# Hybrid decoder layer: the token-major projection and HGRN2 moved ahead of the delta rule, the sample states as moving operands

## The chip, the core and the metric

The kernel runs on one core of one Trainium2 chip. The metric is device time in microseconds of one execution. Five engines work beside each other and wait for one another by semaphores: PE (matrix multiply, with its weight loads PEld), DVE (vector), ACT (scalar and activation), POOL (GpSimd) and SP, which here only issues transfers. Each engine runs its own instructions in a fixed order: an instruction that waits holds up all behind it.

## What is computed

One layer for a prompt of 1024 tokens and for 8 samples of 4 tokens, with the same weights, 1056 tokens in all:

```python
h = rmsnorm(x);  z = h @ w_in          # columns: q k v | a b | out gate A | q f i | out gate B | two branch gates
qkv = silu(causal_conv(q, k, v))       # branch A, gated delta rule, 4 heads of 128 x 128
for chunk:  u = T(v*beta) - T(k*beta*exp(G)) @ S;  o = q*exp(G) @ S + attn @ u;  S = S*exp(Gl) + k^T u
for chunk:  o = q*exp(B) @ S + attn(q, k, decay per channel) @ i                 # branch B, HGRN2
            S = S*exp(Bl) + k^T i
y = per-head rmsnorm(o) * silu(out gate) @ w_branch                              # for A and for B
x += (sigmoid(ga)*y_a + sigmoid(gb)*y_b) @ w_out
x += (silu(conv(h2 @ w_gate)) * (h2 @ w_up)) @ w_down;   rmsnorm
```

T is the inverse of a lower triangular matrix for each chunk of tokens and each head. Each sample starts from its own state S (128 x 128 for each head, 8 samples), and the new states are outputs.

## The kernel before, in words

Dense products are made in three matmuls that keep f32 accuracy: every operand is split into a high and a low part (`split`, lines 82 to 84: a cast on ACT, a subtraction on DVE), and `mm3` (L109 to L111) adds high x high, high x low and low x high. A *dense step* is one call of the fill queue: it fills one bank of PSUM with 24 such matmuls (8 slices of the 1024 features), 352 tokens wide, and evacuates it. `pd` are the banks of dense products, `pm` those of all else. Names that end in hi and lo are the two parts: `hhi`, `hlo` the normed input with features on partitions, `whi`, `wlo` weights, `ohi`, `olo` the two branches' outputs.

The program has these stages.

1. Start. x comes tile by tile (128 tokens), is normed (`norm`: ACT square, DVE, a power on POOL, DVE) and turned by PE transposes (`to_cm`, L186). The first two q/k projections and the a/b columns (`ab_block`, 16 output rows) are made between these tiles.
2. The rest of q, k, v, as dense steps (`fill.drain`).
3. The delta rule in 4 groups of 256 tokens (`gdn_group`), each with two chunks of 128 tokens for 4 heads. A group is a chain: transposes (L694), decay and Gram matrices (L715, L723), which give `UA`; a trip of UA's diagonal blocks through DRAM (`dU`, then `Db`); a forward substitution of 31 dependent pairs of DVE instructions (L749, L751); a second trip through DRAM (`dX`, then `Yd`, transposed to `Xd`); the assembly of T (L773 to L801); two chunk steps on the state (L817 to L835); the head norm (`head_post`, L597 to L612), and a store of the result to `oT_d`.
4. HGRN2 in 4 groups (`hgrn_group`), each a chain of seven levels (`hgrn_attn`: small matmuls L976 or L963, a masked copy on DVE, a product on DVE and one on POOL, then the next level).
5. The dense rest: branch projections, `w_out`, the FFN. It begins with loads of `raw` from `oT_d` (L1151) and splits into `ohi` and `olo`, which lie where `hhi` and `hlo` lay.

In stages 3 and 4 the generators yield numbers, and `drive` runs that many dense steps from the queue `fill` before it goes on. So out gates, HGRN2's projections, the token-major projection of i (`ib_work`, tokens on partitions) and the 16 branch gates lie between the steps of a chain. The samples' own delta rule and HGRN2 run beside the prompt's as a side generator. `sample_products` multiplies each sample's state with its few columns: the state (128 x 128, f32) is the stationary operand, 4 or 8 columns move (L629).

The order in which instructions are written is not the order in which they run: a scheduler orders each engine's instructions by the priority of the writing order, and takes a later one forward where by its own estimate the engine would stand idle. So dense steps are pulled ahead into the long waits.

Of the kernel before, what the change touches and what calls it, by code (L numbers as in the profile page):

```python
# [42 lines left out]
def hybrid_step(ctx: ExitStack, tc: tile.TileContext, ins, outs):  # L43
# [227 lines left out]
    wab = ini.tile([P, KD, 16], F32R, name="wab")  # L271
    rab = ini.tile([P, KD, 8], F32, name="rab")
# [14 lines left out]
    load_x(0)  # L287
    nc.sync.dma_start(out=g_bc, in_=I["g_attn"].broadcast_to([P, D]))
    load_x(1)
    load_x(2)  # L290
    for t in range(3):
        norm1(t)
    W0 = load_w([[(KD, w_in[:, c:c + P])] for c in (OFF_K, OFF_Q)])
    load_x(3)
    load_x(4)
    load_x(5)
    nc.sync.dma_start(out=rab, in_=w_in[:, OFF_AB:OFF_AB + 8].rearrange("(k p) n -> p k n", p=P))
    split(wab[:, :, 0:8], wab[:, :, 8:16], rab)
    abT = ini.tile([16, T], F32, name="abT")

    def ab_block(nb):
        ps = PSD()
        bs = slice(nb * BW, (nb + 1) * BW)
        for k in range(KD):
            if k < KD - 1:
                nc.tensor.matmul(ps[:16, :BW], wab[:, k, :], hhi[:, k, bs], start=k == 0, stop=False)
            nc.tensor.matmul(ps[:8, :BW], wab[:, k, 0:8], hlo[:, k, bs], start=False, stop=False)
        nc.tensor.matmul(ps[:16, :BW], wab[:, KD - 1, :], hhi[:, KD - 1, bs], start=False, stop=True)
        nc.scalar.copy(out=abT[:, bs], in_=ps[:16, :BW])
# [10 lines left out]
    cw = ini.tile([28, 1536], F32, name="cw")  # L320
    nc.sync.dma_start(out=cw[0:24, :], in_=I["cache_conv_qkv"].rearrange("l b t c -> (l b t) c"))
    nc.sync.dma_start(out=cw[24:28, :], in_=I["w_conv_a"].rearrange("l t c -> (l t) c"))
    first = [qkv_work(W0, 0, 0, 0, n1), qkv_work(W0, 1, 1, 0, n1)]
# [3 lines left out]
    cm1(2)
    rowsT(cwT, cw, 12, 28)
    next(first[0])
    norm1(4)  # L330
    load_x(6)
    cm1(3)
    next(first[1])
    norm1(5)
    load_x(7)
    load_x(8)
    cm1(4)
    ab_block(0)
    cm1(5)
    next(first[0])  # L340
    for t in (6, 7):
        norm1(t)
# [205 lines left out]
    def ib_work():  # L548
        for q in range(2):
            hi, lo = w_in_pair(OFF_IB + q * 256, OFF_IB + q * 256 + P)  # L550
            for t in range(NT):
                n = rows(t)
                if t == NC - 1:
                    hs = mp.tile([P, KD, 2 * NS], F32R, name="hs", tag="um", bufs=1)
                    nc.scalar.copy(out=hs[:, :, 0:NS], in_=hhi[:, :, SEQ:].bitcast(F32))
                    nc.scalar.copy(out=hs[:, :, NS:], in_=hlo[:, :, SEQ:].bitcast(F32))
                ps = PSD()
                if t < NC:
                    mm3(ps[:n, :256], hhi[:, :, t * P:t * P + n], hlo[:, :, t * P:t * P + n], hi, lo,
                        [(k, k) for k in range(KD)])  # L560
                    if t % 4 == 0:
                        vt = gp.tile([P, T], F32, name="vt", tag="sl")
                        vt = vt[:, :4 * 256].rearrange("p (t c) -> p t c", c=256)
                    nc.scalar.copy(out=vt[:, t % 4, :], in_=ps[:, :256])
                    if t % 4 == 3:
                        nc.scalar.dma_start(out=vb_d[(t - 3) * P:(t + 1) * P, q * 256:(q + 1) * 256]
                                            .rearrange("(t p) c -> p t c", p=P), in_=vt)
                else:
                    mm_s(ps[:, :256], hs, hi, lo, [(k, k) for k in range(KD)])
                    vt = gp.tile([P, T], F32, name="vts", tag="sl")  # L570
                    nc.scalar.copy(out=vt[:NS, :256], in_=ps[:NS, :256])
                    nc.vector.tensor_tensor(vt[:NS, :256], vt[:NS, :256], ps[NS:2 * NS, :256], ALU.add)
                    for k in range(2):
                        h = 2 * q + k
                        nc.scalar.dma_start(out=vb_s[32 * h:32 * h + 32, :], in_=vt[:NS, k * P:(k + 1) * P])
                    done.add(("vb", q))
                if t != NC - 1:
                    yield

# [11 lines left out]
    def head_post(x, o_sb, ss, eps_t, og, ps_cols):  # L591
# [12 lines left out]
        yield 1.6  # L604
# [68 lines left out]
    def gdn_group(g, St):  # L673
# [88 lines left out]
        yield 3.2  # L762
# [172 lines left out]
    def hgrn_attn(q, f, kk, tots, nch, nlev, attn, ad):  # L935
# [15 lines left out]
        for l in range(nlev):  # L951
# [43 lines left out]
            yield 0.6  # L995
# [53 lines left out]
    def hgrn_sample():  # L1049
# [20 lines left out]
        nc.scalar.copy(out=t1, in_=ps[:, 0:P])  # L1070
# [25 lines left out]
    fill.drain()  # L1096
    for h in (0, 2):
        fill.add(two(OFF_OGA + h * P, OFF_OGA + (h + 1) * P, og_work, (0, h), og_work, (0, h + 1)))
    for h in range(H):
        fill.add(two(OFF_QB + h * P, OFF_FB + h * P, q_work, (h,), f_work, (h,)))  # L1100
    fill.add(ib_work())
    for h in (0, 2):
        fill.add(two(OFF_OGB + h * P, OFF_OGB + (h + 1) * P, og_work, (1, h), og_work, (1, h + 1)))
    for x, off in ((0, OFF_GA), (1, OFF_GB)):
        for d in range(0, KD, 2):
            fill.add(two(off + d * P, off + (d + 1) * P, gate_work, (x, d), gate_work, (x, d + 1)))
# [237 lines left out]
```

## Time and profile before

| | |
|---|---|
| median of 3 runs | 1810.07 us (1806.06 to 1816.28) |
| profiled execution | 1807.24 us, span 1805.5 us |
| PE busy | 1734.0 us, 96% |
| DVE busy | 925.6 us, 51% |
| ACT busy | 524.1 us, 29% |
| POOL busy | 178.9 us, 10% |

The span is what the profiler saw of the instructions; 1.7 us of the execution lie around it. PE's busy time counts from the start of an instruction to its modelled end, so that matmuls overlap; what is missing to the span is time in which PE waited. A group's mean duration is longer than the time from one matmul to the next, which is read from the number of instructions in a stretch that is full.

### The profile page before, as it was taken

To read this page: it belongs to the slowest core of one execution; us is meant where nothing else is said; L and a number is where in the kernel's file an instruction comes from. 1 tells how busy PE (TensorE), PEld (TensorE's weight loads), DVE (VectorE), ACT (ScalarE), POOL (GpSimd) and SP (SyncE) were. 2 spreads that over 40 slices of the span, in tenths; PEclk is the share of its full clock that TensorE was granted. 3 is DMA by queue.
4 is the path that set the end of the run, shared out by engine and by line. 5 is a ranking of instruction groups with operands and counts; after the bars stand their busy time and mean duration, and the time that the engine had idled before them with its cause. 6 is when DMAs were issued, how large, how long until landed. Compare 5 with 4: busy or idle time off the path is not lost.

```text
span 1805.5 us, 30256 instructions
## 1 busy us (share of the span) xinstructions
PE 1734.0 (96%) x12761; PEld 1641.6 (91%) x12761; DVE 925.6 (51%) x1578; ACT 524.1 (29%) x1141; POOL 178.9 (10%) x313
## 2 busy tenths in 40 slices
PE   6999999999999887999999999999999999999998
PEld 5999898989898776999999999989989899899896
DVE  5555555756565456315542634454453453554456
ACT  5533425443343333323110522112112112122122
POOL 2210101111010233200000100000000000000001
PEclk9999999999999999999999999999999999999999
DMA  5333343453324444364432111111111111111102
GB/s 164 85 114 105 108 135 106 133 163 108 108 75 130 129 136 130 109 218 121 139 103 87 55 47 36 54 40 40 43 47 47 47 47 47 47 47 47 47 27 109
DMA packets 199955, 161.81 MB, mean 90 GB/s; under 512 B 17982, under 2 KB 186064, under 8 KB 199801
## 3 DMA queue, kind: packets, MB, share of 16 engines
q1 hardware_dynamic: 175382, 123.92, 23.7%
q10 hardware_dynamic: 24438, 35.96, 5.6%
q8 instruction: 100, 1.64, 0.4%
q14 instruction: 35, 0.29, 0.0%
HBM read 119.57 MB, written 40.21 MB: 88 GB/s over the span
## 4 chain that ended last, share of the span: by engine, by line
PE 55%; DVE 3%; issue 1%; ACT 1%; POOL 1%; POOLq 0%; ACTq 0%; DVEq 0%
PE pd L109 18%; PE pd L110 18%; PE pd L111 18%; PE pd L121 1%; DVE y L177 1%; POOL rs L76 1%; DVE tmp L177 0%; PE pd L120 0%; ACT tmp L174 0%; DVE olo L84 0%; DVE mlo L84 0%; PE pd L123 0%; DVE x L1294 0%; DVE x L1212 0%; PE pm L976 0%
## 5 line engine op out<-in xcount | busy, mean ns | idle before, releaser
L109 PE MATMUL pd<-hhi,whi 128*128 128x352 f32 x1056 | 347.0, 329 | 0.4 <-ACT z L218 0.4
L111 PE MATMUL pd<-hhi,wlo 128*128 128x352 f32 x1056 | 344.9, 327 | 0.0
L110 PE MATMUL pd<-hlo,whi 128*128 128x352 f32 x1056 | 344.8, 327 | 0.0
L109 PE MATMUL pd<-mhi,whi 128*128 128x352 f32 x1056 | 340.5, 323 | 0.0
L110 PE MATMUL pd<-mlo,whi 128*128 128x352 f32 x1056 | 338.6, 321 | 0.7 <-DVE mlo L84 0.7
L111 PE MATMUL pd<-mhi,wlo 128*128 128x352 f32 x1056 | 338.3, 321 | 0.0
L84 DVE TENSOR_TENSOR wlo<-wraw,whi 128x1024 fp32r<-128x1024 f32 x130 | 159.3, 1236 | 205.1 <-ACT whi L83 204.7
L83 ACT CAST whi<-wraw 128x1024 fp32r<-128x1024 f32 x130 | 135.3, 1053 | 409.4 <-PE pd L111 201.9
L109 PEld LDWEIGHTS pd<-hhi,whi 128*128 128x128 f32 x1056 | 199.7, 189 | 2.2 <-ACT z L218 0.7
L110 PEld LDWEIGHTS pd<-hlo,whi 128*128 128x128 f32 x1056 | 200.0, 189 | 1.2 <-DVE hlo L84 0.4
L111 PEld LDWEIGHTS pd<-hhi,wlo 128*128 128x128 f32 x1056 | 199.8, 189 | 0.7
L110 PEld LDWEIGHTS pd<-mlo,whi 128*128 128x128 f32 x1056 | 198.4, 188 | 1.3 <-DVE mlo L84 0.9
L109 PEld LDWEIGHTS pd<-mhi,whi 128*128 128x128 f32 x1056 | 198.0, 188 | 0.4
L111 PEld LDWEIGHTS pd<-mhi,wlo 128*128 128x128 f32 x1056 | 198.1, 188 | 0.0
L1294 DVE TENSOR_TENSOR x<-x,pd 128x512 f32<-128x512 f32 x176 | 119.0, 686 | 78.1 <-PE pd L111 77.8
L109 PE MATMUL pd<-whi,act 128*128 128x512 f32 x352 | 138.1, 392 | 0.1
L110 PE MATMUL pd<-wlo,act 128*128 128x512 f32 x352 | 137.2, 390 | 0.0
L111 PE MATMUL pd<-whi,act 128*128 128x512 f32 x352 | 137.1, 389 | 0.0
L1271 DVE TENSOR_TENSOR ga<-pd,ga 128x352 f32<-128x352 f32 x66 | 34.5, 523 | 98.5 <-PE pd L111 98.5
L218 ACT COPY z<-pd 128x352 f32<-128x352 f32 (+1 forms) x102 | 44.3, 444 | 136.8 <-PE pd L111 128.2
L109 PEld LDWEIGHTS pd<-whi,act 128*128 128x128 f32 x352 | 66.0, 188 | 16.2 <-PE pd L111 1.9
L111 PEld LDWEIGHTS pd<-whi,act 128*128 128x128 f32 x352 | 66.1, 188 | 14.1
(416 smaller groups left out, 2669.1 us busy)
## 6 DMA issues: line engine op xcount, KB each, us to landing
wraw<-in_w_in SPq DMA_DIRECT2D x48, 512.0 KB
wraw<-in_w_ffn_gate SPq DMA_DIRECT2D x22, 512.0 KB
wraw<-in_w_ffn_up SPq DMA_DIRECT2D x22, 512.0 KB
wraw<-in_w_ffn_down SPq DMA_DIRECT2D x22, 512.0 KB
sg_d<-sg ACTq DMA_DIRECT2D x16, 528.0 KB
qkv_d<-sl ACTq DMA_DIRECT2D x12, 512.0 KB
sgb<-sg_d SPq DMA_DIRECT2D x12, 352.0 KB
sga<-sg_d SPq DMA_DIRECT2D x12, 352.0 KB
```

Of the source, the lines that this page charges most:

```text
L76: nc.gpsimd.tensor_tensor(out, in_, pexp[:n, which, :w], ALU.pow)
L83: nc.scalar.copy(out=hi, in_=src)
L84: (eng or nc.vector).tensor_tensor(lo, src, hi.bitcast(F32), ALU.subtract)
L109: nc.tensor.matmul(ps, whi[:, kw], xhi[:, kx], start=q == 0, stop=False)
L110: nc.tensor.matmul(ps, whi[:, kw], xlo[:, kx], start=False, stop=False)
L111: nc.tensor.matmul(ps, wlo[:, kw], xhi[:, kx], start=False, stop=q == n - 1)
L121: nc.tensor.matmul(ps[:NS], st[:, kx, 0:NS], wlo[:, kw], start=False, stop=False)
L177: nc.vector.scalar_tensor_tensor(xn[:n], xt[:n], rs[:n], g_bc[:n], ALU.mult, ALU.mult)
L218: nc.scalar.copy(out=z[:, pad + a:pad + e], in_=ps[:, :e - a])
L1271: nc.vector.tensor_tensor(a[:, bs], ps, a[:, bs], ALU.mult)
L1294: nc.vector.tensor_tensor(x1[:, t, qs], x1[:, t, qs], ps, ALU.add)
```

## The change

Three things are changed, and a few numbers.

- **Order.** The token-major projection of i goes into the start: its 512 columns and the 8 a/b columns are loaded first (`load_ib`, 0.5 MB each), split into `ibw`, and each token tile is multiplied with columns 0 to 263 (i and a/b) and 264 to 519 as soon as it is turned (`ib_tile`). `ab_block`, its weights and its transposes go. Then come HGRN2's q and f, then HGRN2's four groups, then the delta rule's four groups. The fill queue is filled once, in this order: q/f, out gate B, k/q, v, out gate A, branch gates. `raw` is loaded with branch B first.
- **Sample states as moving operands.** `sample_products` lays the samples' columns into a zeroed tile `zc` with a stride of 36, so that a window of 32 columns holds the 4 of one sample and zeros. These 32 columns are stationary, the state's 128 columns move, and the 8 samples accumulate in 32 rows of PSUM for each head. The result comes out with tokens on partitions, so that the transposes of `sT` go. It holds `nk` banks of `pm` and loads one sample with 4 heads at a time.
- **More dense blocks between dependent steps.** HGRN2's levels yield 0.9 and not 0.6, the head norm 2.2 and not 1.6, the second trip through DRAM 3.5 and not 3.2.

```diff
-    def ib_work():
-        for q in range(2):
-            hi, lo = w_in_pair(OFF_IB + q * 256, OFF_IB + q * 256 + P)
...
+    ibw = [ini.tile([P, KD, 520], F32R, name=f"ibw{i}") for i in range(2)]
+    ibc = ((0, 264), (264, 520))
...
+    def ib_tile(t, q):
+        n = rows(t)
+        c0, c1 = ibc[q]
         ps = PSD()
...
+            mm3(pv, hhi[:, :, t * P:t * P + n], hlo[:, :, t * P:t * P + n], *wv, [(k, k) for k in range(KD)])
+            nc.scalar.copy(out=vt[:, t % 2, qs], in_=ps[:, :256])
+            if q == 0:
+                nc.vector.tensor_copy(ab[:, t, :], ps[:, 256:264])
...
-        yield 1.6
+        yield 2.2
...
-        ps = PSM()
-        pv = ps[:, :nk * P].rearrange("p (a h b t) -> p a h b t", a=nk, h=H, t=STEP)
-        for h in range(H):
-            for g in range(2):
-                Sb = sample_load(src, h, g)
-                for b in range(4):
-                    ts = slice(STEP * (4 * g + b), STEP * (4 * g + b + 1))
-                    nc.tensor.matmul(pv[:, :, h, 4 * g + b, :], Sb[:, b, :], cols[:, :, h, ts], start=True, stop=True)
-                yield 0.2
...
+        for b in range(NBAT):
+            Sb, nxt = nxt, load(b + 1) if b + 1 < NBAT else None
+            for a in range(nk):
+                for h in range(H):
+                    nc.tensor.matmul(ps[a][32 * h:32 * h + 32, 0:P], zc[:, a * H + h, 32 * b:32 * b + 32],
+                                     Sb[:, h, :], start=b == 0, stop=b == NBAT - 1, skip_group_check=True)
+            yield 0.2
...
-        yield 3.2
+        yield 3.5
...
-            yield 0.6
+            yield 0.9
...
+    need(*[("qf", k, h) for k in range(2) for h in range(H)])
...
-    St = None
-    side.append(gdn_sample())
-    for g in range(NG):
-        St = drive(gdn_group(g, St))
...
     for g in range(NG):
         St = drive(hgrn_group(g, St, attn, ad))
+    need(*[("qkv", k, h) for k in range(3) for h in range(H)])
+    side.append(gdn_sample())
+    St = None
+    for g in range(NG):
+        St = drive(gdn_group(g, St))
...
-    for x, a, b in ((0, 0, T), (1, 0, last), (1, last, T)):
+    for x, a, b in ((1, 0, T), (0, 0, last), (0, last, T)):
```

The order of PE's instructions at three places follows. Between two levels of HGRN2's third group (L976 before, L971 now), PE before:

```order
L976 MATMUL pm<-qf,kk 32x16 x32
L109 MATMUL pd<-hhi,whi 128x352
L110 MATMUL pd<-hlo,whi 128x352
L111 MATMUL pd<-hhi,wlo 128x352
L109 MATMUL pd<-hhi,whi 128x352
L110 MATMUL pd<-hlo,whi 128x352
L111 MATMUL pd<-hhi,wlo 128x352
L109 MATMUL pd<-hhi,whi 128x352
L976 MATMUL pm<-qf,kk 32x16 x32
```

and now, the first rows of the same place:

```order
L971 MATMUL pm<-qf,kk 32x16 x32
L109 MATMUL pd<-hhi,whi 128x352
L110 MATMUL pd<-hlo,whi 128x352
L111 MATMUL pd<-hhi,wlo 128x352
L109 MATMUL pd<-hhi,whi 128x352
L110 MATMUL pd<-hlo,whi 128x352
L111 MATMUL pd<-hhi,wlo 128x352
L109 MATMUL pd<-hhi,whi 128x352
L110 MATMUL pd<-hlo,whi 128x352
L111 MATMUL pd<-hhi,wlo 128x352
L109 MATMUL pd<-hhi,whi 128x352
L110 MATMUL pd<-hlo,whi 128x352
```

Seven dense matmuls stood between two levels, now 24 do; eleven of them are shown. In the delta rule's last group, at its forward substitution, which ends with L773 (now L768), the first product of the inverse's diagonal blocks `Xd`, PE before:

```order
L110 MATMUL pd<-hlo,whi 128x352
L111 MATMUL pd<-hhi,wlo 128x352
L109 MATMUL pd<-hhi,whi 128x352
L110 MATMUL pd<-hlo,whi 128x352
L111 MATMUL pd<-hhi,wlo 128x352
L109 MATMUL pd<-hhi,whi 128x352
L110 MATMUL pd<-hlo,whi 128x352
L773 MATMUL pm<-Xd,UA 32x32 x16
L111 MATMUL pd<-hhi,wlo 128x352
L109 MATMUL pd<-hhi,whi 128x352
```

and now:

```order
L710 MATMUL pm<-eem,A 128x128 x2
L718 MATMUL pm<-x_7752 128x256 x3
L710 MATMUL pm<-eem,A 128x128 x2
L109 MATMUL pd<-hhi,whi 128x352
L110 MATMUL pd<-hlo,whi 128x352
L111 MATMUL pd<-hhi,wlo 128x352
L718 MATMUL pm<-x_7752 128x256
L768 MATMUL pm<-Xd,UA 32x32 x16
L776 MATMUL pm<-W_8142,Yd 32x32
L779 MATMUL pm<-Yd,W_8142 32x32 x2
L776 MATMUL pm<-W_8142,Yd 32x32
L779 MATMUL pm<-Yd,W_8142 32x32 x2
```

Before, 288 dense matmuls stood between the group's last Gram product (L723) and L773, and 72 more from there to the transposes of the head norm. Now three stand before the last Gram product (L718), none after it: they are the last that read `hhi`. At the end of the last group of stages 3 and 4, where the head norm's transposes (L610, now L597) read `o_sb`, PE before:

```order
L111 MATMUL pd<-hhi,wlo 128x352
L610 MATMUL pm<-ident,o_s 128x128
L610 MATMUL pm<-ident,o_sb 128x128 x8
L109 MATMUL pd<-hhi,whi 128x352
L110 MATMUL pd<-hlo,whi 128x352
L111 MATMUL pd<-hhi,wlo 128x352
L109 MATMUL pd<-hhi,whi 128x352
L110 MATMUL pd<-hlo,whi 128x352
L111 MATMUL pd<-hhi,wlo 128x352
```

and now:

```order
L823 MATMUL pm<-yv,UA 128x128 x4
L828 MATMUL pm<-ut,kvt 128x128 x4
L830 MATMUL pm<-ut,UA 128x128 x4
L597 MATMUL pm<-ident,o_sb 128x128 x8
L245 MATMUL pm<-ident,cout 27x128 x12
L109 MATMUL pd<-ohi,whi 128x352 x2
L110 MATMUL pd<-olo,whi 128x352
L111 MATMUL pd<-ohi,wlo 128x352
L109 MATMUL pd<-ohi,whi 128x352
L110 MATMUL pd<-olo,whi 128x352
```

Before, 17 dense steps of the fill queue (408 matmuls that read `hhi`) followed the last head norm. Now the first dense matmul behind it is the branch projection's, which reads `ohi`.

## Rows read from the trace of the kernel before

**Rows 1.** The page, busy time of PE: us, share of the span, instructions.
```profile
PE 1734.0 (96%) x12761; PEld 1641.6 (91%) x12761; DVE 925.6 (51%) x1578; ACT 524.1 (29%) x1141; POOL 178.9 (10%) x313
```
**Rows 2.** Windows: stretch, us, busy PE PEld DVE ACT POOL, clock, DMA share, GB/s.
```profile
0.00:25.00 25.00, 9.65 (x44) 8.41 (x45) 11.96 (x20) 13.33 (x22) 9.69 (x35) 1.00 0.89 256
100.00:125.00 25.00, 25.00 (x159) 25.00 (x158) 14.82 (x13) 6.92 (x14) 2.71 (x10) 1.00 0.29 90
```
**Rows 3.** Windows: the delta rule's last chain, HGRN2, the dense steps left.
```profile
513.00:588.00 75.00, 72.58 (x566) 70.10 (x564) 44.45 (x109) 22.87 (x55) 5.12 (x11) 1.00 0.40 116
588.00:757.00 169.00, 141.76 (x2494) 128.52 (x2493) 94.80 (x160) 60.15 (x171) 57.20 (x43) 0.97 0.40 123
757.00:823.00 66.00, 65.05 (x409) 64.76 (x408) 6.01 (x7) 12.31 (x22) 0.00 (x0) 1.00 0.57 188
```
**Rows 4.** Waits of PE: what it waited for, us in total, times, longest.
```profile
PE pm L976 <- DVE qf L989: 8.0, 10, 1.2
...
PE pm L694 <- DMA vx<-qkv_d: 2.0, 1, 2.0
```
**Rows 5.** Groups by line: the a/b projection's matmuls.
```profile
L307 PE MATMUL pd<-hlo,wab 128*8 128x352 f32 x24 | 7.2, 321 | 0.0
L306 PE MATMUL pd<-hhi,wab 128*16 128x352 f32 x21 | 6.9, 332 | 0.0
```
**Rows 6.** Timeline of PE: start us, length us, engine, line, tile, count.
```profile
263.69 1.85 PE L629 MATMUL pm<-qkv_s,Sb 128*128 128x8 f32 x16
571.53 1.06 PE L817 MATMUL pm<-St,x 128*128 128x128 f32 x8
588.12 0.76 PE L946 MATMUL pm<-qf,kk 128*32 128x32 f32 x64
```
**Rows 7.** Timeline of the start.
```profile
11.11 1.05 ACT L83 CAST whi<-wraw 128x1024 fp32r<-128x1024 f32 x1 [0.65 <-DMA wraw<-in_w_in]
14.40 1.97 PE L186 MATMUL pm<-ident,xn 128*128 128x128 f32 x8 [4.25 <-DVE ss L175]
21.08 0.96 PE L109 MATMUL pd<-hhi,whi 128*128 128x352 f32 x2
```
**Rows 8.** Timeline of DVE in the delta rule's last chain.
```profile
511.83 1.65 DVE L724 SCALAR_TENSOR_TENSOR UA<-pm,pr,EE 128x256 f32<-128x256 f32 x4
523.51 0.69 DVE L744 TENSOR_SCALAR Db<-Db 128x1024 f32<-128x1024 f32 x1 [3.25 <-DMA Db<-dU]
541.10 1.22 DVE L84 TENSOR_TENSOR wlo<-wraw,whi 128x1024 fp32r<-128x1024 f32 x1
550.19 0.42 DVE L751 TENSOR_REDUCE X<-Pt 128x8 f32<-128x256 f32 x1
558.15 0.45 DVE L763 STREAM_TRANSPOSE Xd<-Yd 128x256 f32<-128x256 f32 x1 [7.54 <-DMA Yd<-dX]
586.26 1.41 DVE L612 SCALAR_TENSOR_TENSOR og<-pm,ga_c,og 128x512 f32<-128x512 f32 x2
```
**Rows 9.** Timeline of the transfers' issues behind the last head norms, and of ohi.
```profile
758.14 0.37 ACTq L1044 DMA_DIRECT2D oT_d<-og  x1
764.58 0.34 SPq L1144 DMA_DIRECT2D x1s<-in_x_sample  x1
823.23 0.48 ACT L83 CAST ohi<-raw 128x352 fp32r<-128x352 f32 x1
```
**Rows 10.** Transfers from 740 to 840 us: GB/s in 40 slices, issues and KB.
```profile
GB/s 109 0 0 105 0 93 192 324 256 14 134 345 384 413 418 393 399 343 262 174 56 0 0 7 189 272 173 1 95 130 136 7 0 135 290 145 0 0 0 35
...
raw<-oT_d SPq DMA_DIRECT2D x1, 2112.0 KB
raw<-oT_d SPq DMA_DIRECT2D x1, 1536.0 KB
```
**Rows 11.** Windows of 4 us around a gap of PE.
```profile
820.00:824.00 4.00, 2.29 (x14) 2.00 (x14) 1.00 (x1) 2.06 (x4) 0.00 (x0) 1.00 0.00 0
824.00:828.00 4.00, 3.63 (x13) 3.34 (x13) 3.71 (x9) 4.00 (x10) 0.00 (x0) 0.58 0.95 276
```

More of the change, by code (lines that the diff above doesn't have):

```diff
@@ L285, in cm1 @@
         to_cm(t, xts.pop(t), (hhi, hlo))
[L287 to L299, printed above, removed]
@@ L301, in ab_block @@
-    def ab_block(nb):
-        ps = PSD()
[L303 to L309, printed above, removed]
+    ibw = [ini.tile([P, KD, 520], F32R, name=f"ibw{i}") for i in range(2)]
@@ new lines, in hybrid_step, with load_ib @@
+    ibc = ((0, 264), (264, 520))
+    ab = const.tile([P, NT, 8], F32, name="ab")
+    vb_s = const.tile([P, P], F32, name="vb_s")
+    nc.gpsimd.memset(ab[:, NC, :], 0.0)
+    hs = ini.tile([P, KD, 2 * NS], F32R, name="hs")
+    vts = {}
+    def load_ib(j):
+        raw = wpool.tile([P, KD, P], F32, name="wraw")
+        c = OFF_IB + j * P
+        nc.sync.dma_start(out=raw, in_=w_in[:, c:c + P].rearrange("(k p) n -> p k n", p=P))
+        cs = slice(j * P + 8 * (j // 2), (j + 1) * P + 8 * (j // 2))
+        return lambda: split(ibw[0][:, :, cs], ibw[1][:, :, cs], raw)
@@ new lines, in ib_tile @@
+    def ib_tile(t, q):
+        n = rows(t)
+        c0, c1 = ibc[q]
+        ps = PSD()
+        pv = ps[:, :c1 - c0]
+        wv = [w[:, :, c0:c1] for w in ibw]
+        qs = slice(q * 256, (q + 1) * 256)
+        if q == 0 and t % 2 == 0:
+            vts["vt"] = gp.tile([P, T], F32, name="vt", tag="sl")[:, :1024].rearrange("p (t c) -> p t c", c=512)
+        vt = vts["vt"]
+        if t < NC:
+            mm3(pv, hhi[:, :, t * P:t * P + n], hlo[:, :, t * P:t * P + n], *wv, [(k, k) for k in range(KD)])
+            nc.scalar.copy(out=vt[:, t % 2, qs], in_=ps[:, :256])
+            if q == 0:
+                nc.vector.tensor_copy(ab[:, t, :], ps[:, 256:264])
+            elif t % 2:
+                nc.scalar.dma_start(out=vb_d[(t - 1) * P:(t + 1) * P, :].rearrange("(t p) c -> p t c", p=P), in_=vt)
+        else:
+            mm_s(pv, hs, *wv, [(k, k) for k in range(KD)])
+            nc.scalar.copy(out=vt[:NS, 0, qs], in_=ps[:NS, :256])
+            nc.vector.tensor_tensor(vt[:NS, 0, qs], vt[:NS, 0, qs], ps[NS:2 * NS, :256], ALU.add)
+            if q == 0:
+                nc.vector.tensor_copy(ab[:NS, NC, :], ps[:NS, 256:264])
+                nc.vector.tensor_tensor(ab[:NS, NC, :], ab[:NS, NC, :], ps[NS:2 * NS, 256:264], ALU.add)
+            for k in range(2):
+                h = 2 * q + k
+                nc.scalar.dma_start(out=vb_s[32 * h:32 * h + 32, :], in_=vt[:NS, 0, h * P:(h + 1) * P])
+            done.add(("vb", q))
@@ L318, in rowsT @@
             nc.vector.tensor_copy(dst[:, k0:k1, :], ps[:, :(k1 - k0) * r].rearrange("p (k r) -> p k r", r=r))
[L320 to L323, printed above, removed]
+    load_x(0)
+    nc.sync.dma_start(out=g_bc, in_=I["g_attn"].broadcast_to([P, D]))
+    sp = [load_ib(0), load_ib(1)]
+    rab = ini.tile([P, KD, 8], F32, name="rab")
+    nc.sync.dma_start(out=rab, in_=w_in[:, OFF_AB:OFF_AB + 8].rearrange("(k p) n -> p k n", p=P))
+    load_x(1)
+    norm1(0)
+    sp[0]()
+    sp[1]()
+    split(ibw[0][:, :, 256:264], ibw[1][:, :, 256:264], rab)
     cm1(0)
+    sp = [load_ib(2), load_ib(3)]
+    load_x(2)
+    norm1(1)
+    ib_tile(0, 0)
     cm1(1)
-    norm1(3)
[L327 to L342, printed above, removed]
+    sp[0]()
+    sp[1]()
+    ib_tile(1, 0)
+    load_x(3)
+    load_x(4)
+    norm1(2)
+    ib_tile(0, 1)
+    ib_tile(1, 1)
+    cm1(2)
+    load_x(5)
+    norm1(3)
+    for t in range(2, NT):
+        ib_tile(t, 0)
+        if t + 1 < NT:
+            cm1(t + 1)
+        if t == NC - 1:
+            nc.scalar.copy(out=hs[:, :, 0:NS], in_=hhi[:, :, SEQ:].bitcast(F32))
+            nc.scalar.copy(out=hs[:, :, NS:], in_=hlo[:, :, SEQ:].bitcast(F32))
+        if t + 4 < NT:
+            load_x(t + 4)
+        if t + 2 < NT:
+            norm1(t + 2)
+        if t == 3:
+            cw = ini.tile([28, 1536], F32, name="cw")
+            nc.sync.dma_start(out=cw[0:24, :], in_=I["cache_conv_qkv"].rearrange("l b t c -> (l b t) c"))
+            nc.sync.dma_start(out=cw[24:28, :], in_=I["w_conv_a"].rearrange("l t c -> (l t) c"))
+        ib_tile(t, 1)
+        if t == 5:
+            rowsT(cwT, cw, 12, 28)
     fw = ini.tile([19, FF], F32, name="fw")
@@ L546, in gate_work @@
         nc.scalar.dma_start(out=sg_d[x][d], in_=t)
-    def ib_work():
-        for q in range(2):
-            hi, lo = w_in_pair(OFF_IB + q * 256, OFF_IB + q * 256 + P)
[L551 to L578, printed above, removed]
     def pair(c0, c1, f0, f1):
@@ L1069, in hgrn_sample @@
         t1 = T1("t1h", "t1_s")
-        nc.scalar.copy(out=t1, in_=ps[:, 0:P])
+        nc.scalar.copy(out=t1, in_=ps[0])
         po = PSM()
@@ L1086, in two @@
         return pair(off0, off1, lambda W, j: f0(W, j, *a0), lambda W, j: f1(W, j, *a1))
-    for h in range(1, H):
+    for h in range(H):
+        fill.add(two(OFF_QB + h * P, OFF_FB + h * P, q_work, (h,), f_work, (h,)))
+    for h in (0, 2):
+        fill.add(two(OFF_OGB + h * P, OFF_OGB + (h + 1) * P, og_work, (1, h), og_work, (1, h + 1)))
+    for h in range(H):
         fill.add(two(OFF_K + h * P, OFF_Q + h * P, qkv_work, (0, h), qkv_work, (1, h)))
@@ L1091, in hybrid_step @@
         fill.add(two(OFF_V + h * P, OFF_V + (h + 1) * P, qkv_work, (2, h), qkv_work, (2, h + 1)))
+    for h in (0, 2):
+        fill.add(two(OFF_OGA + h * P, OFF_OGA + (h + 1) * P, og_work, (0, h), og_work, (0, h + 1)))
+    for x, off in ((0, OFF_GA), (1, OFF_GB)):
+        for d in range(0, KD, 2):
+            fill.add(two(off + d * P, off + (d + 1) * P, gate_work, (x, d), gate_work, (x, d + 1)))
     fill.step()
@@ L1095, in hybrid_step @@
             fill.step()
[L1096 to L1106, printed above, removed]
+    need(*[("qf", k, h) for k in range(2) for h in range(H)])
     side = []
```

49 lines of the change are left out of this document (16 added, 33 removed).

## Prediction

> **What bounds the kernel now.** The page comes first: PE is busy for 1734.0 of 1805.5 us [rows 1], so that little but PE's work and PE's waits can change the time. Windows come second, to see what a full stretch looks like and where it is not full. From 100 to 125 us 159 dense matmuls fill 25.0 us [rows 2]: 157 ns each at full clock, and 3.77 us for a dense step of 24. PE is far from full in three places. In the first 25 us it is busy for 9.65 [rows 2], so 15.35 us are lost. In HGRN2, from 588 to 757 us, it is busy for 141.76 of 169 [rows 3]: 27.2 us lost, and the mean granted clock is 0.97. Elsewhere it is nearly full. In the delta rule's last chain only 2.4 of 75 us are lost, and in the 66 us behind HGRN2 only 0.95 [rows 3]. The third view is the order of PE's instructions, which says what makes these two stretches full: dense steps of the fill queue, 288 + 72 matmuls in the first and 408 in the second. The sum of the dense steps is the same in both kernels. The question is thus which waits they cover.
>
> **The change part by part.** I sum against the profiled execution, 1807.24 us, 1.7 above its span and 2.8 below the median shown.
>
> *The a/b projection.* Its 24 + 21 matmuls [rows 5] are 352 wide and cost 157 ns each as all such: -7.1 us. In their place 208 matmuls of the token-major projection are 8 columns wider, 8/352 of 157 ns: +0.7. Nothing hides either, both are PE's own work: -6.4 us. The matmuls of i themselves only move.
>
> *The sample states.* Before, 16 instructions take 1.85 us, 116 ns each, and there are 128: 14.8 us of PE. Now 96 products are 192 instructions (f32 takes two), each with 32 stationary and 128 moving columns. No row has that shape. Full-width f32 instructions with 128 moving columns start 112 ns apart (8 in 1.06 us, the last one's 0.28 taken off), which would make 21.5 us, 6.7 more than before. The level matmuls L946 have 32 stationary columns in four strips of the array and 32 moving: 64 in 0.76 us, the last one's 0.20 off, 9 ns apart [rows 6]. At four times the columns that is 28 (a quarter of 112) to 36 ns. I take 32 ns, 6.1 us, since the new products walk through the four strips as L946 does: -8.7, and -0.7 for the three transposes of `sT`. Together -9.4 us, between -10 and +6.
> The Trainium skill, TensorEngine Tiling (Array Packing), Key Properties, says that tiles of the array work independently and in parallel; the 9 ns of L946 agree. By that rule it is a quarter of 112 ns, which is my lower end; without it the upper.
>
> *The start.* Before, the first dense matmul runs at 21.08 us, because a block of 352 tokens needs three turned tiles. Now it needs one tile, whose transposes come as before, and weights which before were cast at 11.11 us [rows 7] behind two more tiles of x; now they are ahead of these. But POOL still makes its constants before the second tile's power, so that this tile's transposes stay near 14.40 us [rows 7], and in the new order they stand inside the first tile's 24 matmuls. From then on a tile is 48 matmuls and 8 transposes, about 6.5 us, which ACT and DVE (about 3 us of casts, norms and copies each) can feed. So PE gains what it does between 12 and 21 us less its stops: 3 us, between 0 and 6.
>
> *HGRN2.* In its first group the order leaves 5 to 11 dense matmuls between most levels, as before; in the other three 13 to 24 where 7 stood, and 72 before the head norm. Between two levels PE stops up to 1.2 us for DVE's product, 0.8 in the mean [rows 4], behind 7 dense matmuls of 1.1 us; so a level takes 1.9 to 2.3 us, and 12 to 15 dense matmuls cover it. I keep 4.5 us of stops in the first group and 3.5 in the others of the 27.2: -19 us. The clock's 0.03 of 169 us comes back for the most part: -4. Bounds -12 and -32 (all of it).
>
> *New boundaries.* HGRN2 now starts on `qf_d` just written, as the delta rule did on `qkv_d` for a wait of 2.0 us [rows 4]; and the delta rule still does: +2. In the delta rule's first group all 64 sample products stand between the steps of T and of the state, with 37 dense matmuls where 76 stood, and wait for 8 loads in turn, two at a time: +4 (0 to 12). The other two groups keep their 250 to 290 dense matmuls per substitution: 0.
>
> *The delta rule's last group.* This is the largest term. Before, it runs from the last Gram products, whose results are in `UA` at 513.5 us, to 523.5 (`Db` there), 550.6 (substitution done), 558.15 (`Xd`) and 587.7 (`og` done) [rows 8]: 75 us, of which PE fills 72.6 [rows 3]. The 360 dense matmuls are 56.5 us of that, the chain's own products 16. Now no dense matmul is left: the queue is empty, and the branch projection reads what this chain makes. The chain itself gets shorter only by what dense work did to it: two weight splits of 1.2 us inside the substitution (one is shown [rows 8]) and some 2.7 us of dense matmuls and casts queued ahead of its links. So 70 us, plus 2.5 for its products at the lower clock after so long a wait. Of 72.5 us PE has 16 to do: 56.5 idle where 2.4 were, +54 us. Lower bound 46 (trips through DRAM, alone, 7 us shorter), upper 62 (all 16 us of products at half clock).
>
> *The way to the branch projection.* Before, the store of `oT_d` is issued at 758.14 us, the loads of `raw` behind x1s at 764.58 [rows 9], which waits for all users of the pool; and dense steps cover everything until `ohi` at 823.23. Now nothing does. From `og` on: 7.5 us to that issue (6.4 and the stores of the conv cache, which also lie there), then 2112 + 1536 KB before branch A's first columns are there, 9 us at the 400 GB/s of the 40 slices' fullest ones [rows 10], and 2 of latency, then a cast and a subtraction, 1. That is 19.5 us, less the 2 that PE loses there today (1.7 from 820 to 824 us [rows 11] and a little behind it): +18, between 13 and 23. The low clock behind the gap is no new cost: it is there today [rows 11].
>
> **Sum:** -6.4 - 9.4 - 3 - 23 + 6 + 54 + 18 = +36.2 us, a span of 1841.7 and an execution of 1843 us.
>
> **Rivals.**
> 1. *The clock stays low.* Behind 1.7 us without work PE's clock is 0.58 for 4 us [rows 11], which is the lower of the two levels for most of it. If it is low for all of the last chain, its 16 us of products cost up to 16 more on the critical path, of which I have 2.5; about 10 of them are links: +8, 1851 us. For it: the chain has gaps throughout. Against: HGRN2 with its gaps of about 1 us keeps 0.97 [rows 3].
> The Trainium skill, TensorE: Matmul & The Clock Gate, Part 1, says that the array is throttled by default and that activity releases it. The 0.58 behind the gap agrees; by that rule alone the chain, which is more gap than work, would run at the low level, and this rival's 1851 would hold.
> 2. *The strips don't overlap* at 128 moving columns: +15, 1858 us. Against it stand the 9 ns.
> 3. *HGRN2 doesn't gain*, since DVE and POOL set a level's time however PE is fed: 23 us become 5, 1861 us. Against it: where PE stops, it stops for the level's own result, 0.8 us in the mean.
> 4. *Not slower.* Alone on its engines, the last chain is much shorter than where it shared them. It decides if chain and way to the branch together take less than 55 us and not 92, since the other terms give back 36. But the substitution alone is 24 us of back-to-back DVE instructions, the links from `Xd` to `og` 26, and 3.6 MB must come in: these leave nothing. With every term at its good end the sum is +5, 1812 us.
>
> **How the numbers follow.** Chances: forecast 0.72, rival 1 0.10, rival 2 0.07, rival 3 0.06, rival 4 0.05. The forecast's own range is 1826 to 1858, from the bounds of the last chain (-8, +8), the way (-5, +5), HGRN2 (-9, +7) and the samples' loads, which won't all fall on one side. Rivals 1 to 3 end within 1861; the range is 1822 to 1861. A change under 0.5% (9 us) can't be told from none here. Rival 4 gives 0.02 for faster and 0.03 for the same: 0.02, 0.04 with a little for chance, 0.94 slower.
>
> **What would show it.** In the profile after, a gap of about 45 us on PE, whose releaser is DVE's `Xd`, with the forward substitution in it, then a stretch where PE is busy for a half or less, then a gap of about 20 us that ends with `ohi`; HGRN2 with under 10 us of stops; the sample products about 30 ns apart; the first dense matmul before 14 us. Wrong: if dense matmuls lie in that gap, if chain and way together take under 75 us, or if PE's stops before the last group add up to over 45 us.

## The result and the profile after

The changed kernel takes 1867.76 us (median of 4 runs, 1866.14 to 1871.3) against 1808.07 for the kernel before on the same chip (1802.62 to 1816.28): 1.0329 times as long, interval 1.0285 to 1.0373. The forecast had the sign and the two largest terms, but 1843 us and a range that ended at 1861 were too low. The profiled execution is 58.9 us longer than that of before (1866.14 against 1807.24), where the sum said 36.2.

PE's busy time has hardly changed; what was added is waiting, and stretches at a lower clock. First the page's line on busy time:

```profile
span 1864.4 us, 30256 instructions
PE 1738.4 (93%) x12765; PEld 1644.4 (88%) x12765; DVE 927.8 (50%) x1585; ACT 526.4 (28%) x1140; POOL 187.5 (10%) x315
```

PE is idle for 126.0 us instead of 71.5 [rows 1]. What it waited for in the first 900 us (total, times, longest):

```profile
PE pm L768 <- DVE Xd L758: 52.6, 4, 42.4
PE pd L109 <- ACT ohi L83: 18.0, 1, 18.0
PE pm L597 <- DVE o_sb L590: 9.6, 5, 5.4
PE pm L186 <- DVE xn L177: 7.8, 1, 7.8
PE pm L971 <- POOL z L213: 6.3, 3, 4.2
PE pm L971 <- DVE qf L984: 3.1, 4, 1.1
PE pd L109 <- ACT hhi L83: 2.3, 1, 2.3
PE pm L958 <- POOL z L213: 2.1, 1, 2.1
```

Of the 52.6 us behind `Xd`, 42.4 are the bare last chain that was forecast. The other 10.2 are three stops of up to 3.8 us in the delta rule's first three groups, which were not. The windows say what came with them (PE busy, loads, DVE, ACT, POOL, granted clock, DMA, GB/s):

```profile
core 0: us, PE busy (x) PEld busy (x) DVE busy (x) ACT busy (x) POOL busy (x), PEclk, DMA share, GB/s
0.00:25.00 25.00, 14.71 (x92) 13.55 (x93) 13.92 (x22) 14.11 (x23) 11.14 (x32) 1.00 0.96 290
375.00:400.00 25.00, 20.78 (x415) 19.39 (x414) 19.35 (x26) 8.10 (x20) 13.10 (x14) 0.93 0.42 133
400.00:425.00 25.00, 22.86 (x185) 21.85 (x183) 17.97 (x24) 10.06 (x30) 6.45 (x10) 0.93 0.45 125
525.00:550.00 25.00, 21.17 (x227) 16.84 (x226) 4.61 (x9) 3.47 (x9) 1.08 (x3) 0.66 0.38 110
530.00:545.00 15.00, 15.00 (x164) 11.47 (x161) 3.48 (x7) 0.46 (x1) 0.55 (x2) 0.50 0.28 88
625.00:650.00 25.00, 21.81 (x214) 19.56 (x213) 9.97 (x20) 6.51 (x14) 1.08 (x3) 0.86 0.35 97
725.00:750.00 25.00, 21.86 (x191) 20.11 (x190) 13.71 (x26) 5.18 (x10) 0.78 (x2) 0.81 0.33 96
750.00:775.00 25.00, 24.53 (x166) 23.25 (x166) 9.07 (x24) 7.38 (x29) 1.94 (x2) 0.85 0.24 79
800.00:825.00 25.00, 0.00 (x0) 0.00 (x0) 20.59 (x61) 0.00 (x0) 0.16 (x1) 0.50 0.14 34
825.00:850.00 25.00, 13.78 (x157) 12.94 (x158) 7.66 (x20) 3.33 (x9) 0.78 (x2) 0.57 0.06 11
850.00:875.00 25.00, 8.88 (x57) 7.55 (x55) 6.30 (x15) 6.33 (x24) 1.64 (x1) 0.70 0.25 79
875.00:900.00 25.00, 15.99 (x89) 15.54 (x90) 15.35 (x25) 9.41 (x17) 0.00 (x0) 0.75 0.58 213
```

Behind each stop for `Xd` the clock is well under 1.00 (0.66, 0.86, 0.81 and 0.85), though PE is nearly always busy there. In the kernel before it was 1.00 in all four substitutions and their links, from 220 to 588 us:

```profile
220.00:588.00 368.00, 355.92 (x2775) 341.78 (x2773) 218.75 (x530) 136.98 (x380) 42.92 (x60) 1.00 0.41 121
```

The products that run in these stretches are links of the chain. In DVE's timeline of group 0, from `Xd` to the normed head outputs:

```profile
528.91 0.45 DVE L758 STREAM_TRANSPOSE Xd<-Yd 128x256 f32<-128x256 f32 x1 [6.59 <-DMA Yd<-dX]
537.12 0.69 DVE L792 COPY XW<-pm 64x512 f32<-64x512 f32 x1 [2.02 <-PE pm L791]
541.95 0.68 DVE L797 TENSOR_SCALAR UA<-pm 64x512 f32<-64x512 f32 x1 [4.13 <-PE pm L796]
555.11 1.12 DVE L838 SCALAR_TENSOR_TENSOR St<-St,eGl,pm 128x128 f32<-128x128 f32 x4 [3.77 <-PE pm L828]
562.02 2.14 DVE L590 TENSOR_TENSOR o_sb<-o_sb,pss 128x512 f32<-128x512 f32 x2 [1.76 <-POOL pss L76]
```

and in PE's timeline the products for two of them, at the low level:

```profile
535.12 1.97 PE L791 MATMUL pm<-XW,UA 64*64 64x64 f32 x16
537.59 0.66 PE L111 MATMUL pd<-hhi,wlo 128*128 128x352 f32 x1
538.05 0.49 PE L109 MATMUL pd<-hhi,whi 128*128 128x352 f32 x1
538.35 0.49 PE L110 MATMUL pd<-hlo,whi 128*128 128x352 f32 x1
539.94 1.97 PE L796 MATMUL pm<-UA,XW 64*64 64x64 f32 x16
```

Dense matmuls start 290 to 300 ns apart here, not 157. From `Xd` to the normed outputs it is 34.8, 30.5 and 32.6 us in the first three groups; in the kernel before 25.1, 28.7 and 25.8: +18.4 us. From the last `UA` of the first group to that of the last it is 311.8 us instead of 292.7.

The last group went as forecast:

```profile
791.07 1.65 DVE L719 SCALAR_TENSOR_TENSOR UA<-pm,pr,EE 128x256 f32<-128x256 f32 x4
802.08 0.69 DVE L739 TENSOR_SCALAR Db<-Db 128x1024 f32<-128x1024 f32 x1 [6.74 <-DMA Db<-dU]
826.03 0.42 DVE L746 TENSOR_REDUCE X<-Pt 128x8 f32<-128x256 f32 x1
832.90 0.45 DVE L758 STREAM_TRANSPOSE Xd<-Yd 128x256 f32<-128x256 f32 x1 [6.44 <-DMA Yd<-dX]
862.27 1.60 DVE L599 SCALAR_TENSOR_TENSOR og<-pm,ga_c,og 128x512 f32<-128x512 f32 x2 [0.60 <-PE pm L597]
```

From `UA` (792.72) to `og` (863.87) are 71.2 us, where the forecast had 72.5 and the kernel before 74.2 [rows 8]. The casts of `ohi` begin at 878.82, and the branch projection's first matmul runs 4.8 us later:

```profile
883.62 0.95 PE L109 MATMUL pd<-ohi,whi 128*128 128x352 f32 x2 [17.98 <-ACT ohi L83]
```

From `og` to it are 19.75 us, where the forecast had 19.5.

### The profile page after: what moved, and what is told of

The parts are those of the page before. It is cut to its first block, busy times and chain, and to the rows that moved or that the text cites. A ratio compares the mean times of both kernels' runs of the same rounds, so it can differ in the third digit from the quotient of the medians.

```text
span 1864.4 us, 30256 instructions
## 1 busy us (share of the span) xinstructions
PE 1738.4 (93%) x12765; PEld 1644.4 (88%) x12765; DVE 927.8 (50%) x1585; ACT 526.4 (28%) x1140; POOL 187.5 (10%) x315
## 4 chain that ended last, share of the span: by engine, by line
PE 53%; DVE 5%; ACT 2%; DMA 1%; issue 1%; POOL 1%; SPq 0%; ACTq 0%; POOLq 0%; DVEq 0%
PE pd L109 16%; PE pd L110 16%; PE pd L111 16%; DVE Pt L744 1%; DVE X L746 1%; PE pd L121 1%; POOL rs L76 1%; DVE y L177 1%; DVE tmp L177 0%; DMA raw<-oT_d 0%; PE pd L120 0%; ACT tmp L174 0%; PE pm L812 0%; DVE mlo L84 0%; PE pd L123 0%
## 5 line engine op out<-in xcount | busy, mean ns | idle before, releaser
L109 PE MATMUL pd<-hhi,whi 128*128 128x352 f32 x1056 | 351.3, 333 | 0.0
L84 DVE TENSOR_TENSOR wlo<-wraw,whi 128x1024 fp32r<-128x1024 f32 x126 | 153.3, 1227 | 198.0 <-ACT whi L83 197.5
L83 ACT CAST whi<-wraw 128x1024 fp32r<-128x1024 f32 x126 | 130.5, 1049 | 399.1 <-PE pd L111 201.9
L109 PEld LDWEIGHTS pd<-whi,act 128*128 128x128 f32 x352 | 66.1, 188 | 16.2 <-PE pd L111 2.0
L109 PE MATMUL pd<-ohi,whi 128*128 128x352 f32 x192 | 62.6, 327 | 18.0 <-ACT ohi L83 18.0
```

Source lines behind the costliest of these rows:

```text
L83: nc.scalar.copy(out=hi, in_=src)
L84: (eng or nc.vector).tensor_tensor(lo, src, hi.bitcast(F32), ALU.subtract)
L109: nc.tensor.matmul(ps, whi[:, kw], xhi[:, kx], start=q == 0, stop=False)
```

## The experiments

Theory A: PE's stops of some 4 us ahead of `Xd` halve its clock, and the links of groups 0 to 2, which run just behind, get longer. B: the chain on DVE sets these groups' length, and the clock costs nothing. C: the clock falls for the many small f32 products themselves.

**Idle matmuls ahead of Xd, and in the empty queue.**

```diff
         yield 3.5
+        if g < NG - 1:
+            pj = PSM()
+            for k in range(9):
+                nc.tensor.matmul(pj[:, 0:256], ident, X.rearrange("p s r -> p (s r)"), start=k == 0, stop=k == 8)
```

> The changed kernel with 9 idle matmuls more in each of the delta rule's groups 0 to 2 (ident x X, 128x256, f32, result unused; some 4 us of PE), which can start when the substitution's X is done and so lie where PE waits 3.8 us for Xd now. Theory A (the missing 25 us before the last group are mostly a clock that falls behind these waits and stays low for some 20 us): granted clock of 525-550, 625-650, 725-775 us back from 0.66, 0.86 and 0.81/0.85 to 0.95 or more; 12 us of work added, 10 us of waits taken, 12 to 15 us of clock given back: 1850 to 1858 us. Theory B (a group's chain on DVE sets its length, so PE's clock there costs nothing): clock back or not, the time stays at 1864 to 1872 us. Theory C (the clock falls for another reason than the wait, as the many small f32 products behind Xd): clock stays at 0.66 to 0.86, time 1868 to 1880 us.

> The same in all four groups, and wherever the fill queue is empty in the last group idle dense matmuls (hhi x hhi, result unused; 36 for a step ahead of Xd, 12 behind it). Theory A: the last chain runs at a clock near 1.00 instead of 0.50 to 0.70; its 16 us of products, now 71.2 us from UA to og, get shorter by 5 to 10 us, less up to 4 us for idle matmuls queued ahead of links, and the first 25 us of the branch projection are no longer at 0.75 (3 to 4 us): 1840 to 1850 us. Theory B (the last chain is set by DVE and transfers, its clock is worth under 2 us): UA to og 70 us or more, time within 3 us of the run with idle matmuls in three groups only.

They took 1868.55 and 1869.39 us: no gain, which by itself speaks for B. But the edit did more than fill the wait. The idle matmuls stand ahead of 41 dense ones, and PE now stops for X in their place and comes late to the links. In the first run's PE timeline of group 0, `Xd` being there at 530.45:

```profile
521.09 6.52 PE L761 MATMUL pm<-X,ident 128*128 128x256 f32 x18 [4.96 <-DVE X L746]
534.08 0.69 PE L772 MATMUL pm<-Xd,UA 32*32 32x32 f32 x32
537.47 1.14 PE L795 MATMUL pm<-XW,UA 64*64 64x64 f32 x16
```

The clock was back (0.98 from 525 to 550 us), and L795, the same products as L791 above, took 1.14 us instead of 1.97. From the first product behind `Xd` to the second new state it was 19.8 us (534.08 to 553.84), where the changed kernel needs 26.8 (529.41 to 556.23). The 7 us were spent on coming 3.6 us late and on later waits. So the links do follow the clock, but the time is inconclusive. In the second run the clock did not hold either (0.66 from 825 to 850 us), and the last chain's stretch from `UA` to the normed outputs was 67.2 us against 67.5 in the first run: what the low clock costs the last chain stays open. In the changed kernel this chain, with no dense matmul between its links and the clock at 0.50 until 846 us, took 28.3 us from `Xd` to the normed outputs; the kernel before, with dense matmuls between them and 1.00, took 27.5.

**The same wait in pieces.**

```diff
             if r % 8 == 0:
+                if g < NG - 1:
+                    pj = PSM()
+                    nc.tensor.matmul(pj[:, 0:32], ident, X[:, 0, :], start=True, stop=True)
                 yield 0.7
```

> The changed kernel with three tiny matmuls more in the substitution of groups 0 to 2 (ident x 32 columns of X after its steps 8, 16 and 24, result unused), so that PE, which now stops once for 3.8 us ahead of Xd's products, stops earlier and in pieces; the 281 to 294 dense matmuls ahead of Xd stay, nothing is added but 0.1 us each. Theory A (behind a stop of some 4 us the clock is at half for some 15 us, and the links from Xd to the head norm, which run just then, take 26.8 us in group 0 where they took 19.8 us with the clock at 1.00): the clock of these links 0.9 or more, the stretch from Xd to the normed head outputs 26 to 30 us in groups 0 and 2 instead of 34.8 and 32.6, time 1850 to 1860 us. Theory C (the clock falls for the many small f32 products themselves): clock and time as before the edit, 1864 to 1872 us.

1851.88 us (1851.12 to 1853.79), 15.9 less than the changed kernel. Its waits and windows:

```profile
PE pm L771 <- DVE Xd L761: 43.1, 2, 42.8
PE pm L750 <- DVE X L746: 6.5, 8, 1.2
```

```profile
525.00:550.00 25.00, 24.68 (x325) 21.52 (x324) 6.94 (x18) 6.93 (x21) 1.08 (x3) 1.00 0.58 177
625.00:650.00 25.00, 24.99 (x263) 23.25 (x262) 13.47 (x31) 9.73 (x34) 1.57 (x4) 1.00 0.53 151
725.00:750.00 25.00, 24.99 (x259) 23.09 (x258) 10.38 (x24) 9.51 (x27) 1.08 (x3) 1.00 0.38 112
```

Three stops of up to 3.8 us have become eight of up to 1.2, the clock stays at 1.00, and from `Xd` to the normed outputs it is 27.8, 27.1 and 25.8 us. B and C fall: neither the chain's DVE work nor its products were touched. PE's other work in this stretch is the same too: 37, 71 and 66 dense matmuls without the edit, 37, 67 and 66 with it, and the sample products in the first group, so that another order of work doesn't explain it. This is the step that the forecast lacked.

**Delta rule first.** The two recurrences change places again (with the fill queue's order and the loads of `raw`); in the second run also the old numbers:

```diff
-        yield 3.5
+        yield 3.2
...
-            yield 0.9
+            yield 0.6
```

(and 1.6 for 2.2).

> The changed kernel with the delta rule's four groups ahead of HGRN2's again (and k, q, v, out gate A ahead of HGRN2's q, f in the fill queue; raw loaded with branch A first); start, sample states and yields as changed. Theory A (which recurrence comes last decides): the exposed last chain becomes HGRN2's last group, of 42 us with stops of 1 us at most, not 71 us with one of 42: clock about 1.00 up to the end of HGRN2, the way to the branch projection still bare (15 to 20 us): 1792 to 1806 us. Rival (dense work is short: the start now uses up the projection of i, 432 matmuls, which covered waits before; whichever recurrence comes last runs bare): HGRN2 at 25 to 35 us of stops and a low clock in its last two groups, 1815 to 1835 us.

> The delta rule first as in the run before of that order, and the old numbers of dense steps (0.6, 1.6, 3.2). The order of PE's instructions then has 288 dense matmuls in every substitution as there, dense work in HGRN2's last group again and 48 left behind it. Theory (the new numbers only use up dense work that is missing later, since the start has used up i's 432 matmuls): the bare end of HGRN2 (waits and half clock from 775 to 850 us) goes and its earlier groups stop more: 1805 to 1815 us, against 1822. Rival (the delta rule's longer groups, 101.7 us instead of 94.9, come from the start or the samples and stay): groups of 101 us, 1815 to 1825 us.

1822.40 us (1.0058 to 1.0124 times the kernel before), the rival's case: HGRN2's last group runs bare.

```profile
775.00:800.00 25.00, 10.74 (x289) 8.43 (x287) 18.58 (x32) 8.09 (x31) 8.04 (x6) 0.65 0.69 210
800.00:825.00 25.00, 14.53 (x235) 13.02 (x235) 12.02 (x22) 10.04 (x33) 9.60 (x8) 0.67 0.26 74
```

With the old numbers 1807.88 us, as the theory had it, and the same as the kernel before (0.9972 to 1.0013). What is left there:

```profile
PE pd L109 <- ACT ohi L83: 18.8, 1, 18.8
...
PE pm L768 <- DVE Xd L758: 8.5, 3, 4.5
```

So the start's gain (5 us, and 6 for the a/b projection) is paid for at the other end: i's matmuls lie in the start now and no longer cover the way to the branch projection, which is bare for 18.8 us. Its groups 1 and 2 have stops of up to 4.5 us for `Xd` and take 34.6 and 33.1 us behind it, as A says. The rival's long groups stayed as well, 103 us in the mean from one `UA` to the next, though the time is the theory's.

> The kernel with the delta rule first and the old numbers (1807.9 us), with the three tiny matmuls in the substitution of all four groups. Theory A (a long stop ahead of Xd halves the clock of the links behind it): from Xd to the normed outputs 26 to 28 us in every group instead of 25.9, 34.6, 33.1 and 27.8, so 12 to 16 us less: 1792 to 1797 us. Rival (its groups are long for another reason): 1804 to 1809 us.

1803.54 us: the links are back at 27.6, 28.5, 25.7 us and the clock of the profiled delta rule at 1.00, but 4.3 us are gained in the medians, not 12 to 16, and against the kernel before no gain is shown (0.9973 to 1.0011 of it, without the edit 0.9972 to 1.0013). The edit has a price: the substitutions, from their first sum to their last, grow from 28.4, 27.1, 26.0 and 27.8 us to 28.5, 28.4, 28.0 and 30.9.

**Sample states alone, and HGRN2's number.** The kernel before with the new `sample_products`; then also with 0.9 and 1.0 for 0.6 in HGRN2's levels; then 0.9 with the tiny matmuls in all groups.

> The kernel before with nothing but the new sample products (states as moving operands). If the term of -9.4 us holds (192 instructions some 25 to 32 ns apart instead of 128 that are 116 ns apart): 1795 to 1802 us. Rival (the products lie beside waits of the recurrences, and what they free is only more idle time): 1804 to 1811 us.

> The kernel before with the new sample products and with 0.9 instead of 0.6 dense steps between HGRN2's levels, no more. 264 dense matmuls (41 us) stay behind HGRN2 instead of 456, which is enough for the 20 us of the way to the branch projection. Theory (the wait that more dense steps cover is real, it was only paid for with the last chain in the changed kernel): HGRN2's last two groups lose 5 to 9 us of stops: 1789 to 1795 us against 1798. Rival (POOL and DVE set a level's time): 1796 to 1801 us.

> The kernel before with the new sample products, 0.9 in HGRN2, and the three tiny matmuls in all four groups. Theory A: PE's waits for Xd are short here already and the clock of the delta rule is 1.00, so there is nothing to give back: 1790 to 1796 us, the same as without. Rival (tiny matmuls help by themselves, for instance by another order of the dense steps): 1780 to 1788 us.

> The kernel before with the new sample products and 1.0 (not 0.6, nor 0.9) dense steps between HGRN2's levels: 192 dense matmuls (30 us) stay behind HGRN2, where 264 do at 0.9. Theory: the third group's levels get 24 dense matmuls as the fourth's did, 2 to 4 us of stops fewer, and 30 us still cover the 20 us of the way to the branch projection: 1788 to 1793 us. Rival (what is left of the stops is POOL's and DVE's own time, and the cover of the way gets thin): 1793 to 1800 us.

1798.41 us with the sample products alone (0.9944 to 0.9979 of before), 1792.70 with 0.9 (0.9890 to 0.9936) and 1788.74 with 1.0 (0.9878 to 0.9925), the fastest of all and 18.4 us under the kernel before in its runs; the last two intervals overlap. HGRN2 from 590 to 750 us in that one:

```profile
590.00:750.00 160.00, 145.35 (x2511) 132.14 (x2510) 86.59 (x143) 53.98 (x146) 49.32 (x38) 0.99 0.45 138
```

14.7 us of stops, where the sample products alone leave 26.3 (busy 133.69 of the same 160). The way to `ohi` stays covered (one stop of 1.7 us). With 0.9 and the tiny matmuls it took 1802.28 us, 9.6 more than without: both theories missed. The substitutions grow from 28.7, 27.1, 26.5 and 27.1 us to 28.8, 28.3, 28.9 and 30.6, while the clock had been 1.00 already. In the run with the wait in pieces they had hardly grown (23.8, 32.5 and 29.2 us in the changed kernel, 24.3, 32.0 and 29.3 there); why they do here stays open.

The run with 1.0 shows, too, that a short stop can be enough. Its delta rule stops for `Xd` once, for 1.36 us in group 1, and behind it the clock is low:

```profile
365.00:377.00 12.00, 12.00 (x106) 10.84 (x105) 6.24 (x12) 4.01 (x10) 1.34 (x2) 0.50 0.26 87
```

From `Xd` to the normed outputs this group takes 33.1 us; with 0.9, where the stop is 0.93 us and the clock stays at 1.00, 27.9.

**What holds HGRN2.**

```diff
-        nc.gpsimd.memset(z[:, 0:pad], 0.0)
-        nc.gpsimd.tensor_copy(zs[:, :, 0:pad], cacheT.rearrange("p (b t) -> p b t", t=pad))
+        nc.vector.memset(z[:, 0:pad], 0.0)
+        nc.vector.tensor_copy(zs[:, :, 0:pad], cacheT.rearrange("p (b t) -> p b t", t=pad))
```

(and the two copies to the conv cache); in the other run HGRN2's `og` in a tile of its own:

```diff
-        og = mp.tile([P, H, GW], F32, name="og", tag="z")
+        og = mp.tile([P, H, GW], F32, name="og", bufs=1)
         nc.sync.dma_start(out=og, in_=og_d[1][:, :, gs].rearrange("h p t -> p h t"))
```

> The changed kernel with the convolution's small copies (z's edges, conv cache; lines 212, 213, 225, 226) on DVE instead of POOL. Theory: HGRN2's level products on POOL queue behind these copies, which wait for the k/q/v steps that HGRN2 now has as its fill; PE's 8.4 us of waits that are put down to POOL's z (6.3 and 2.1) go, the clock of 375-425 us goes from 0.93 to 1.00: 5 to 9 us less, 1858 to 1863 us. Rival (DVE then holds the levels' own products instead, PE waits for DVE qf): no gain, 1865 to 1872 us.

> The changed kernel with HGRN2's out gate (og, L. 1035) in a tile of its own, where it shared two buffers with the convolutions' z and co. In the changed kernel co's first product waits there 2.6 us for the store of og, and four co passes of 1.3 us then stand ahead of a level's product on DVE. Theory (HGRN2's missing gain is the k/q/v convolutions' work on DVE and its waits, now that k, q and v fill HGRN2): the waits of L971 and L958 put down to z fall from 8.4 to under 5 us, 2 to 5 us less: 1862 to 1866 us. Rival (the store isn't what holds DVE, the passes themselves are): waits as before, 1866 to 1870 us.

Off POOL: 1867.89 us, no gain; the waits for z were 5.6 us, now put down to DVE's z. POOL's queue alone was not the cause. With `og` on its own: 1847.11 us, 20.7 less (1.0229 times the kernel before instead of 1.0329), but not where the theory looked. The delta rule starts where it did (its first group's copies of `kvt` end at 464.1 us, before the edit at 464.5), and all of the gain lies behind:

```profile
PE pm L768 <- DVE Xd L758: 48.1, 4, 43.1
```

Three stops for `Xd` now make 5.0 us together instead of 10.2, the clock is 0.86 from 525 to 550 us and 1.00 in the later groups, and behind `Xd` it takes 27.0, 27.7 and 25.7 us. That is A once more, by another road; why the edit shortens these stops is not settled (another order of the scheduler's is possible, not shown). For HGRN2 the theory falls: its waits for z are 5.5 us instead of 8.4, but those for `qf` 5.5 instead of 3.1. What the trace of the changed kernel shows at HGRN2's longest stop (PE waits until 388.46) is this on DVE:

```profile
382.04 1.34 DVE L231 SCALAR_TENSOR_TENSOR co<-z,cwT,co 128x1080 f32<-128x1080 f32 x1
383.90 1.52 DVE L231 SCALAR_TENSOR_TENSOR co<-z,cwT,co 128x1080 f32<-128x1080 f32 x1
385.57 2.13 DVE L231 SCALAR_TENSOR_TENSOR co<-z,cwT,co 128x1080 f32<-128x1080 f32 x1
387.63 0.68 DVE L984 TENSOR_TENSOR qf<-qf,tots 128x512 f32<-128x512 f32 x1
```

The level's product L984 stands behind the convolution that each k/q/v step brings to DVE. It is read, not tested.

## Why the prediction was wrong in size

*The a/b projection and the start* (-6.4 and -3): PE is busy for 14.71 of the first 25 us, 5.1 more than before [rows 2], and the first dense matmul runs at 12.07. Slightly better than forecast; the a/b part was not measured alone (its 45 matmuls leave out three on L308, 0.5 us).

*The sample states* (-9.4): right in kind. Alone they give 7.3 us (interval 4 to 10). At full clock 16 instructions take 0.65 us, some 25 ns apart, just under the lower end of 28 to 36. The rule of the Trainium skill (TensorEngine Tiling (Array Packing), Key Properties), that tiles of the array work in parallel, agrees.

*HGRN2* (-23): too large. Between 175 and 425 us PE stops for 14.2 us, not 8, and the clock is 0.93 for 50 us. The working counted dense matmuls between the levels, but not what the k/q/v steps do on DVE and POOL; that these are the cause is read from the trace alone.

*New boundaries* (+6): the step that failed, in the words "the other two groups keep their 250 to 290 dense matmuls per substitution: 0". The numbers were right and were never held against the length of what they cover. 281 to 291 matmuls at 157 ns are 44 to 46 us; from `UA` to `Xd` it takes 47.3 to 48.8 in these groups. PE is bare for 3.1 to 3.8 us each time, in the kernel before for 0.9 to 1.3, and the clock halves for what follows. (The sample loads, for which 4 us stood, made PE wait for 0.9.) Taking the other terms as measured, this one is some 22 us and not 6: 58.9 less -6.4, -7.3, -5.1, -14 (27.2 of stops to 14.2, and the clock 0.93 of 50 us where it was 0.97 of 169), 52.7, 18.2 and -1.0. The wait in pieces gives 15.9 of that back by itself.

*The last group* (+54): right. 71.2 us, with a stop of 42.4 that was to be about 45; the 75 us of the kernel before are 74.2 by the prediction's own rows. *The way* (+18): right, 19.75 us where it had 19.5. "The low clock behind the gap is no new cost" held: from the branch projection's first matmul to the end it takes 980.8 us, before 981.8.

Of the signs that were to show the forecast right, HGRN2 with under 10 us of stops did not come; of the signs of being wrong one did: PE's stops up to the last group's `UA` add up to 46.0 us, just over 45.

*Rival 1* named the mechanism and put it in the wrong place. The last chain ran at 0.50 to 0.70 and was no longer for it than forecast; the cost was in the three groups ahead, for which 0.97 with stops of about 1 us [rows 3] had been read as safe. Stops for `Xd` of 0.9 to 1.3 us kept 1.00 in the kernel before; those of 3.1 to 3.8 were each followed by 0.50. In between the runs don't agree: behind 1.36 us the clock fell to 0.50 in one, behind 1.65 and 1.77 us it stayed at 1.00 in another. The Trainium skill (TensorE: Matmul & The Clock Gate, Part 1) says that the array is throttled by default and that activity releases it. The fall behind these stops agrees, and the question should have been asked of every wait, not of the largest. *Rivals 2 to 4* did not come; rival 3 holds in part, as HGRN2 shows.

## What to carry to other kernels

Count cover in microseconds against the chain that it has to cover, wait by wait: 44 us of dense work over 48 us of chain lost far more than the 4. Dense work is a stock: what a faster start uses up is missing at the end, and a last dependent chain needs work beside it that doesn't wait for its result. When a fill step moves beside another chain, what it brings to the vector engines may count as well; here that was read, not tested.

## What was not expected of the hardware

A stop of 3.83 us of PE was followed by a granted clock of 0.50 from 530 to 545 us, though PE was busy without a break from 529.4; eight stops of up to 1.2 us left it at 1.00, and one of 1.36 us in another kernel was followed by 0.50 from 365 to 377 us. Three tiny matmuls in a substitution, 0.1 us each, made it up to 3.5 us longer in one kernel and at most 0.4 in another.
